# A decoder in split-float products: half of the first FFN by seven block products, one tile of convolution moved to ScalarE and GpSimd

## Chip, core and metric

The kernel runs on one core of a Trainium2 chip. The metric is the time of one execution in microseconds of device time. The kernel before takes 2612.85 us, the median of 3 runs (2611.65 to 2614.08).

## What is computed

A trunk of two layers on 1024 tokens of width 1024, float32 in and out. Layer 0 has a causal depthwise convolution of 31 taps, layer 1 forgetting attention with 16 heads. Both end in an FFN with squared ReLU (inner width 4096) and a per-layer gate.

```python
def layer(i, h):                                  # layer 0: conv, layer 1: attention
    hn = rmsnorm(h, mix_norm[i])
    if i == 0:
        a, g = split(hn @ w_pw1 + b_pw1)
        u = depthwise_causal_conv31(a * sigmoid(g)) + b_dw
        h = h + silu(layernorm(u)) @ w_pw2 + b_pw2
    else:
        h = h + forgetting_attention(hn, w_q, k, v, c) @ w_o   # k, v, c from h
    hn = rmsnorm(h, ffn_norm[i])
    h = h + square(relu(hn @ w1[i])) @ w2[i]      # 1024 -> 4096 -> 1024
    gate = sigmoid(rmsnorm(h, ple_norm[i]) @ w_gate[i])
    return h + gate * (p[i] @ w_proj[i])
```

## The kernel before

Activations lie with channels on the partitions, as 8 tiles of 128 channels, and the tokens in two halves of 512. A product of float32 matrices is made of three matmuls on rounded parts (`mm3`, L132): high by high, high by low, low by high. A weight panel (`panel`, L114) is one 512 KB load into a buffer `raw`, a rounding `wh` on ScalarE, and the remainder `wl = raw - wh`, on GpSimd for half 0 and on VectorE for half 1 (`self.subs`). `work_pools` (L89) gives three buffers each to `wh` and `wl`, and by default two to `raw`. One panel serves 24 matmuls of 128x512 per half. `linear` (L143) runs over panels.

`first` is layer 0. `glu` makes the gated product u; `taps` makes the convolution, per channel tile a sum of 31 shifted products on VectorE (lines L332 to L337, two partial sums `ya`), except the tile in `ONPOOL`, whose products ScalarE makes (`cm`) and GpSimd adds (L324). In this kernel that is done for half 0 alone. `ln_silu` (from L340) has the layer norm: `acc_m`, a mean by matmul `cs_m`, the squares in `acc_ln`, the statistics `st_ln`, `r_ln`, `bc_ln`, then the scaled y and its rounded parts `x1h`, `x1l`. `pw2` (`ps_pw`) is the pointwise product after it. `ffn` works on one half at a time in four chunks of 8 inner tiles: `ps_fa` (into the squared ReLU, parts r) and `ps_fb` (back, added to hT). So one half takes 4 x (192 + 192) matmuls. The gate product (`ple`, `ps_gt`) takes both halves with 8 panels.

The second FFN (`ffn_both`, `ffn_in`, `ffn_out`) makes each 2x2 block product in seven instead of eight block products (`seven`): operands x1 to x7 are sums of quarter blocks of the normalized tokens (`z0f` of half 0, `z1f` of half 1, split into `xf`), weights are combined into `wa` and `wb`; products land in `psa` and `psb`, and sums `e` pass through DRAM (`rd`, `rx`). x1 and x2 need half 0 alone, x5 and the rest need both halves; `tokens_first` and `tokens_rest` make them.

The order on each engine is made by a list scheduler from program order and priorities (`tc.high_priority`), within the limits of the buffers. A pool opened for a later scope takes space that a closed one gave back.

Of the kernel before, what the change touches and what calls it, by code (L numbers as in the profile page):

```python
# [59 lines left out]
class K:  # L60
# [313 lines left out]
    def ffn(self, hT, l, halves=(0, 1), sub=None):  # L374
# [78 lines left out]

    def tokens_rest(self, hT, x, f, hd, gain, name):

        nc = self.nc
        nc.sync.dma_start(hd[1], hT[1].rearrange("p k t -> p (k t)"))
        xd = self.dr.tile([P, 2, 4, HB], F32, name=f"xd_{name}")
        bc = self.stats(hT, 1, name)[1]
        g = self.slot([P, 2, 4, HB], F32, f"z1{name}")  # L460

        def new(p, src):
            t = self.block(f"x{name}{p}")
            x[p] = self.parts(src, t[:, 0], t[:, 1])
# [670 lines left out]
```

## Time and profile before

| what | value |
|---|---|
| median of 3 runs | 2612.85 us (2611.65 to 2614.08) |
| profiled execution, its own time | 2616.24 us |
| its span | 2614.5 us |
| mean granted TensorE clock | 0.969 |
| TensorE busy | 2457.6 us (94%) |
| VectorE busy | 1778.6 us (68%) |
| ScalarE, GpSimd busy | 1078.3 us (41%), 913.1 us (35%) |

The profile is of one execution. The chain of waits is followed from the last instruction back, at each step to what released it; a piece on the chain is time of the kernel, a long busy time beside it is not. Lines are those of the kernel before.

### The profile page before, as it was taken

The page shows a single profiled execution, that of the slowest core. Times are in us where ns is not written, and L with a number is a line of the kernel's source. Part 1 is how long each engine was busy: PE and PEld are TensorE (multiplying, and loading weights), DVE is VectorE, ACT ScalarE, POOL GpSimd, SP SyncE. Part 2 cuts the span into 40 slices and gives each one's busy share as a digit, 9 for nine tenths or more (in the row PEclk, how much of TensorE's full clock was granted, in tenths as well). Part 3 has the DMA queues.
Part 4 walks back from the last instruction along what each step waited for, and adds up shares of the span by engine and source line. Part 5 has one row for each costly group of instructions (what it writes and reads, how often), then busy time and mean ns, then how long its engine had stood idle before and what let it go on. Part 6 is the DMA issues. An engine that isn't in the chain of part 4 may idle for free.

```text
span 2614.5 us, 31465 instructions
## 1 busy us (share of the span) xinstructions
PE 2457.6 (94%) x11672; PEld 2053.1 (79%) x11672; DVE 1778.6 (68%) x2723; ACT 1078.3 (41%) x1670; POOL 913.1 (35%) x747
## 2 busy tenths in 40 slices
PE   7997899999999999989999999798799999999996
PEld 6885678888888888878989898677578887888875
DVE  7999999524744345555686867765877669656655
ACT  5245433233432234334566565643433334333432
POOL 3465544444100000001676665640232323555400
PEclk9998899999999999998999999899799999999987
DMA  3125123222223222222111112314254367443032
GB/s 128 49 71 183 57 78 105 97 97 98 92 89 105 97 97 93 101 83 88 62 57 50 51 49 73 107 59 167 97 208 154 141 212 267 153 145 121 36 125 113
DMA packets 101145, 278.14 MB, mean 106 GB/s; under 512 B 9840, under 2 KB 15600, under 8 KB 99584
## 3 DMA queue, kind: packets, MB, share of 16 engines
q1 hardware_dynamic: 99840, 271.94, 30.1%
q10 hardware_dynamic: 1152, 4.19, 0.4%
q8 instruction: 92, 1.51, 0.2%
q14 instruction: 61, 0.50, 0.1%
HBM read 219.93 MB, written 56.16 MB: 106 GB/s over the span
## 4 chain that ended last, share of the span: by engine, by line
PE 76%; DVE 14%; issue 3%; ACT 3%; POOL 2%; DMA 2%; DVEq 0%; SPq 0%; POOLq 0%; ACTq 0%
PE ps_fb L137 13%; PE ps_fa L137 12%; PE psb L137 9%; PE psa L137 8%; PE ps_gt L137 7%; PE ps_wo L137 3%; PE psq L137 3%; DVE ya L332 3%; PE psv L137 3%; PE pg L137 3%; PE psk L137 3%; PE pa L137 3%; PE po L1002 2%; PE t L1032 2%; PE ps_pw L137 2%
## 5 line engine op out<-in xcount | busy, mean ns | idle before, releaser
L137 PE MATMUL psb<-rx,wb 128*128 128x512 f32 x1344 | 308.3, 392 | 5.7 <-ACT wb L111 5.7
L137 PEld LDWEIGHTS psb<-rx,wb 128*128 128x128 f32 x1344 | 254.0, 189 | 59.5 <-ACT wb L111 6.1
L137 PE MATMUL psa<-xf,wa 128*128 128x512 f32 x1200 | 281.4, 396 | 16.8 <-DVE xf L112 5.5
L332 DVE SCALAR_TENSOR_TENSOR ya<-u,wdw,ya 128x512 f32<-128x512 f32 x420 | 284.2, 747 | 0.0
L137 PEld LDWEIGHTS psa<-xf,wa 128*128 128x128 f32 x1200 | 228.4, 191 | 68.2 <-DVE xf L112 6.6
L111 ACT CAST wh_fb<-raw_fb 128x1024 fp32r<-128x1024 f32 x64 | 67.2, 1053 | 213.3 <-PE ps_fb L137 134.3
L111 ACT CAST wh_fa<-raw_fa 128x1024 fp32r<-128x1024 f32 x64 | 67.3, 1052 | 205.8 <-PE ps_fa L137 114.5
L390 DVE TENSOR_TENSOR hT<-ps_fb,hT 128x512 f32<-128x512 f32 x64 | 44.1, 689 | 147.8 <-PE ps_fb L137 147.8
L984 POOL TENSOR_SCALAR pr<-pr,sm 128x896 f32<-128x896 f32 (+7 forms) x128 | 100.0, 783 | 99.9 <-DVE sm L983 93.7
L205 POOL TENSOR_TENSOR r_g<-ms_g,mhalf 128x4 f32<-128x4 f32 x4 | 5.3, 1327 | 368.2 <-DVE ms_g L203 368.2
L112 DVE TENSOR_TENSOR pt<-t,pt 128x512 fp32r<-128x512 f32 (+1 forms) x160 | 99.2, 634 | 48.6 <-ACT pt L111 47.5
L1002 PE MATMUL po<-pt,V 128*128 128x256 f32 x640 | 121.7, 306 | 10.3 <-ACT pt L111 8.4
L112 POOL TENSOR_TENSOR wb<-rwb,wb 128x1024 fp32r<-128x1024 f32 x32 | 87.2, 2734 | 95.9 <-ACT wb L111 86.6
L982 ACT ACTIVATE pr<-pr,sm 128x896 f32<-128x896 f32 (+7 forms) x128 | 99.3, 776 | 51.9 <-DVE sm L981 35.0
L976 DVE CUSTOM_DVE_ANT_0 pr<-s,pr 128x512 f32<-128x512 f32 (+2 forms) x192 | 103.5, 551 | 22.9 <-POOL pr L963 12.8
L962 POOL TENSOR_SCALAR pr<-cb,ctok 128x896 f32<-128x896 f32 (+7 forms) x128 | 104.9, 826 | 36.1 <-PE t L1032 30.5
L384 DVE SCALAR_TENSOR_TENSOR fa<-ps_fa,bs_f 128x512 f32<-128x512 f32 x64 | 43.8, 689 | 108.4 <-PE ps_fa L137 105.0
L111 ACT CAST pt<-t 128x512 fp32r<-128x512 f32 (+1 forms) x160 | 84.0, 539 | 74.3 <-PE t L1032 70.9
L112 POOL TENSOR_TENSOR wl_fb<-raw_fb,wh_fb 128x1024 fp32r<-128x1024 f32 x32 | 77.4, 2420 | 104.0 <-ACT wh_fb L111 104.0
L112 POOL TENSOR_TENSOR wl_fa<-raw_fa,wh_fa 128x1024 fp32r<-128x1024 f32 x32 | 79.1, 2474 | 90.8 <-ACT wh_fa L111 90.8
L112 DVE TENSOR_TENSOR rx<-rx 128x1024 fp32r<-128x1024 f32 x56 | 79.9, 1437 | 41.8 <-ACT rx L111 41.8
L1002 PEld LDWEIGHTS po<-pt,V 128*128 128x128 f32 x640 | 92.8, 196 | 18.7 <-ACT pt L111 12.4
(362 smaller groups left out, 7094.7 us busy)
## 6 DMA issues: line engine op xcount, KB each, us to landing
raw_fa<-in_wf SPq DMA_DIRECT2D x64, 512.0 KB, 3.4
raw_fb<-in_wf SPq DMA_DIRECT2D x64, 512.0 KB, 3.5
rd<-e SPq DMA_DIRECT2D x112, 256.0 KB, 2.5
rx<-rd SPq DMA_DIRECT2D x28, 1024.0 KB, 5.6
rwa<-in_wf SPq DMA_DIRECT2D x32, 512.0 KB, 4.7
rwb<-in_wf2s SPq DMA_DIRECT2D x32, 512.0 KB, 4.3
raw_gt<-in_wgate SPq DMA_DIRECT2D x24, 512.0 KB, 3.5
proj<-pj SPq DMA_DIRECT2D x32, 256.0 KB, 2.4
```

The costliest lines, as they stand in the source:

```text
L111: copy(h, src)
L112: sub.tensor_tensor(l, src, h.bitcast(F32), ALU.subtract)
L137: self.nc.tensor.matmul(ps, p[:, k, :], q[:, k, :], start=(start and k == k0 and n == 0), stop=(stop and k == kt - 1 and n == 2), skip_gro ...
L332: nc.vector.scalar_tensor_tensor(d, s(j), w(j), o, ALU.mult, ALU.add)
L384: nc.vector.scalar_tensor_tensor(t, ps, 0.0, s[h][1], ALU.max, ALU.mult)
L390: nc.vector.tensor_tensor(hT[h][:, j, :], ps, hT[h][:, j, :], ALU.add)
L962: nc.gpsimd.tensor_scalar(z, cb[:, 0:W], -1.0, self.ctok[:, i, n : n + 1], ALU.mult, ALU.add)
L976: nc.vector.tensor_tensor_reduce(zz, ps[:, 0 : hi - lo], zz, -1.0, 3.0e38, ALU.add, ALU.min, sm[:, m : m + 1])
L982: nc.scalar.activation(z, z, AF.Exp, bias=sm[:, 0:1], scale=-1.0, accum_out=sm[:, 2:3])
L984: nc.gpsimd.tensor_scalar(z, z, sm[:, 3:4], 1.0, ALU.mult, ALU.mult)
L1002: nc.tensor.matmul(po, V[:, j, n % 4, :], pt[:, q, c : c + 256], start=(j == 0 and q == 0), stop=(jp == u and jj == 1 and q == 1),)
L1032: nc.tensor.transpose(ps[:, c : c + P], pr[b][:, j * P : (j + 1) * P], self.ident)
```

## The change

In the first FFN only chunks 0 and 1 (`PLAIN`) stay as they were, for each half. The other 16 inner tiles are made by `ffn_both` with both halves together, with n = 8 and weights stored anew (`wf2s0`). For that the tokens of each half before the FFN are stored to DRAM (`hp`, 2 MB a half) and fetched again, and those after the plain chunks too (`hq`). The plain matmuls fall from 3072 to 1536, and 1344 are added in blocks: 192 fewer in all.

The convolution of half 1 uses `ONPOOL` too: the 32 VectorE instructions of one channel tile become ScalarE products and 30 GpSimd sums. `first` has two pool scopes. The second, with the layer norm, pw2 and plain FFN of half 1, has **one** raw buffer in place of two (and 3 temporaries in place of 4). The gate product of layer 0 takes the halves one after the other, with 16 panel loads in place of 8.

At the end of attention the norm and the operands x1, x2 of half 0 for the second FFN are made in attention's own scope, ahead of the last output products of half 1; and the scope of those last 8 panels has one raw buffer and one temporary.

```diff
+PLAIN = (0, 1)
...
-    def ffn(self, hT, l, halves=(0, 1), sub=None):
+    def ffn(self, hT, l, halves, chunks, sub=None):
...
-        for c in range(NCH):
+        for c in chunks:
...
-            self.linear(a["wf2"][l, c], KT, r, evac2, f"fb{tag}{c}", **kw)
+            self.linear(a["wf2"][c], KT, r, evac2, f"fb{tag}{c}", **kw)
+        return s
...
-    def tokens_first(self, hT, gain, name):
-
-        hd = self.dr.tile([NH, P, KT * HB], F32, name=f"hd_{name}")
-        self.nc.sync.dma_start(hd[0], hT[0].rearrange("p k t -> p (k t)"))
-        bc = self.stats(hT, 0, name)[1]
-        f = self.slot([P, 2, 4, HB], F32, f"z0{name}")
+    def keep(self, dst, hT):
+        self.nc.sync.dma_start(dst, hT.rearrange("p k t -> p (k t)"))
+
+    def tokens_first(self, src, bc, gain, name):
+
+        f = self.slot([P, KT, HB], F32, f"z0{name}")
+        src = self.fetch(f, src)
+        f = f.rearrange("p (i k) t -> p i k t", i=2)
         x = {}
         for p, i in ((1, 0), (2, 1)):
-            self.norm4(f[:, i], hT[0], gain, 4 * i, bc)
+            self.norm4(f[:, i], src, gain, 4 * i, bc)
             t = self.block(f"x{name}{p}")
             x[p] = self.parts(f[:, i], t[:, 0], t[:, 1])
-        return hT, x, f, hd, gain, name
-
-    def tokens_rest(self, hT, x, f, hd, gain, name):
-
-        nc = self.nc
-        nc.sync.dma_start(hd[1], hT[1].rearrange("p k t -> p (k t)"))
+        return x, f, gain, name
+
+    def fetch(self, f, src):
+        if len(src.shape) == 3:
+            return src
+        self.nc.sync.dma_start(f.rearrange("p k t -> p (k t)"), src)
+        return f
+
+    def tokens_rest(self, x, f, gain, name, src, bc):
+
+        nc = self.nc
         xd = self.dr.tile([P, 2, 4, HB], F32, name=f"xd_{name}")
-        bc = self.stats(hT, 1, name)[1]
-        g = self.slot([P, 2, 4, HB], F32, f"z1{name}")
-
-        def new(p, src):
+        g = self.slot([P, KT, HB], F32, f"z1{name}")
+        src = self.fetch(g, src)
+        g = g.rearrange("p (i k) t -> p i k t", i=2)
+
+        def new(p, s):
             t = self.block(f"x{name}{p}")
-            x[p] = self.parts(src, t[:, 0], t[:, 1])
+            x[p] = self.parts(s, t[:, 0], t[:, 1])
...
-            self.norm4(g[:, 1], hT[1], gain, 4, bc)
+            self.norm4(g[:, 1], src, gain, 4, bc)
...
-        self.norm4(g[:, 0], hT[1], gain, 0, bc)
+        self.norm4(g[:, 0], src, gain, 0, bc)
...
-    def ffn_both(self, l, first):
+    def ffn_both(self, l, x, hd, t0, n, w2, rest, pair):
...
-        rd = self.dr.tile([8, 16, P, HB], F32, name=f"rd{l}")
+        rd = self.dr.tile([8, n, P, HB], F32, name=f"rd{l}")
...
-            sp = self.pool(c, f"sw{l}", 2)
-            wr = self.pool(c, f"wr{l}", 4)
-            hT, x, _, hd, gain, name = first
+            sp = self.pool(c, f"sw{l}", 2, side="right")
+            wr = self.pool(c, f"wr{l}", 4, side="right")
...
+                gs = [(0, 1)] if pair else [(0,)]
+                gs += [(g,) for g in range(len(gs[0]), n // 2)]
+                for i, g in enumerate(gs):
+                    for j in g:
+                        load(j)
+                    self.ffn_in(l, g, raw, sp, x, rd, None if i else between)
...
-                for c in range(4):
-                    self.ffn_out(l, c, hT, load_h, wr, wq, sp, rd)
+                for c in range(n // 4):
+                    self.ffn_out(l, c, hT, load_h, wr, wq, sp, rd, w2, c == n // 4 - 1)
...
-                yB = self.taps(u, 1)
+                yB = self.taps(u, 1, ONPOOL)
                 back = tc.cur_priority - p0
             self.sqp = None
+            hp = self.dr.tile([NH, P, KT * HB], F32, name="hp")
+            hq = self.dr.tile([NH, P, KT * HB], F32, name="hq")
             with tc.high_priority(offset=back + 3000):
                 self.pw2(hT, x1, 0)
-                self.ffn(hT, 0, (0,), sub=nc.gpsimd)
-            self.sqp, self.sqt = self.tp, "bc"
+                self.keep(hp[0], hT[0])
+                s0 = self.ffn(hT, 0, (0,), PLAIN, sub=nc.gpsimd)[0]
+                self.keep(hq[0], hT[0])
+        with ExitStack() as c1:
+            self.work_pools(c1, 4, 1, 3)
+            self.psum_pools(c1, 4)
+            self.sqt, self.sqp = "sq", self.pool(c1, "sq0", 3)
             x1 = self.ln_silu(yB, 1)
             self.pw2(hT, x1, 1)
-            self.sqt, self.sqp = "sq", self.pool(c1, "sq0", 3)
-            self.ffn(hT, 0, (1,))
-            self.ple(hT, 0, pj0)
-        return pj1
+            self.keep(hp[1], hT[1])
+            first = self.tokens_first(hp[0], s0[1], "ffn0", "f0")
+            s1 = self.ffn(hT, 0, (1,), PLAIN)[1]
+            self.keep(hq[1], hT[1])
+            late = self.tokens_rest(*first, hp[1], s1[1])
+        hT = self.ffn_both(0, first[0], hq, KT * len(PLAIN), FF // P // 2 - 4 * len(PLAIN), self.a["wf2s0"], lambda: late, False)
+        with ExitStack() as c1:
+            self.work_pools(c1, 5)
+            self.psum_pools(c1, 5)
+            self.sqt, self.sqp = "sq", self.pool(c1, "sq5", 3)
+            self.ple(hT, 0, pj0, (1, 0))
+        return hT, pj1
...
+            hf = self.dr.tile([NH, P, KT * HB], F32, name="hf")
             for k0, k1, h in ((0, KSPLIT, 0), (KSPLIT, NP, 0), (0, KSPLIT, 1)):
                 for _ in self.out_product(k0, k1, (h,), self.at):
                     pass
-                if k0 == 0 and h == 0:
+                if h == 0 and k0 == 0:
                     for p in range(KSPLIT, NP - 1):
                         self.load_o(od, p)
+                elif h == 0:
+                    with tc.high_priority(offset=1):
+                        self.keep(hf[0], self.hn[0])
+                        first = self.tokens_first(self.hn[0], self.stats(self.hn, 0, "f1")[1], "ffn1", "f1")
         with ExitStack() as c3:
-            self.work_pools(c3, 2)
+            self.work_pools(c3, 2, 1, 1)
             self.psum_pools(c3, 2)
             self.sqp = None
-            first = self.tokens_first(self.hn, "ffn1", "f1")
             for _ in self.out_product(KSPLIT, NP, (1,)):
                 pass
-        return first
+        return self.hn, hf, first
...
-        pj1 = k.first(hT)
-        hT = k.ffn_both(1, k.attention(hT))
+        hT, pj1 = k.first(hT)
+        hT, hf, first = k.attention(hT)
+
+        def rest():
+            k.keep(hf[1], hT[1])
+            return k.tokens_rest(*first, hT[1], k.stats(hT, 1, "f1")[1])
+
+        hT = k.ffn_both(1, first[0], hf, 0, 16, a["wf2s1"], rest, True)
```

Three places show how the rows move. The first is TensorE at the end of half 0's plain FFN, around the mean `cs_m` of half 1's layer norm; before:

```order
L137 MATMUL ps_fb_0_4626<-r03h_4298,wl_fb_4623 128x512
L137 MATMUL ps_fb_0_4658<-r03h_4298,wh_fb_4654 128x512
L137 MATMUL ps_fb_0_4658<-r03l_4299,wh_fb_4654 128x512
L349 MATMUL cs_m_4852<-acc_m_4844,meanm 128x512 [waits DVE_49,PE_49]
L137 MATMUL ps_fb_0_4658<-r03h_4298,wl_fb_4655 128x512 [waits Pool_49]
L137 MATMUL ps_fb_0_4658<-r03h_4298,wh_fb_4654 128x512
```

and now, with the statistics and the first matmul of pw2 (`ps_pw_1`):

```order
L141 MATMUL ps_fb_0_3786<-r01l_3267,wh_fb_3782 128x512
L141 MATMUL ps_fb_0_3786<-r01h_3266,wl_fb_3783 128x512
L353 MATMUL cs_m_3840<-acc_m_3832,meanm 128x512 [waits DVE_49]
L193 MATMUL st_ln_3850<-meanm,acc_ln_3851 128x1 [waits DVE_49]
L193 MATMUL st_ln_3850<-meanm,acc_ln_3851 128x1 x3
L162 MATMUL bc_ln_3882<-ident,r_ln_3880 128x128 [waits Pool_49]
L162 MATMUL bc_ln_3882<-ident,r_ln_3880 128x128 x3
L141 MATMUL ps_pw_1_3943<-x1h_3919,wh_pw_3939 128x512 [waits Activation_49]
```

The mean stood among the products of chunk 3; now it stands behind the last product of half 0, and nothing of another stage stands between it and pw2. On VectorE, in the same place, the sum `acc_m` before:

```order
L112 TENSOR_TENSOR r03l_4299<-fa_4547,r03h_4298 128x512 [waits Activation_49]
L384 SCALAR_TENSOR_TENSOR fa_4583<-ps_fa_0_4558,bs_f_2658 128x512 [waits DVE_49,PE_49]
L344 TENSOR_TENSOR acc_m_4844<-y_2072 128x512 [waits DVE_49]
L346 TENSOR_TENSOR acc_m_4844<-acc_m_4844,y_2072 128x512 [waits DVE_49]
L112 TENSOR_TENSOR r03l_4299<-fa_4583,r03h_4298 128x512 [waits Activation_49]
L346 TENSOR_TENSOR acc_m_4844<-acc_m_4844,y_2072 128x512 [waits DVE_49] x5
L390 TENSOR_TENSOR hT_87<-ps_fb_0_4594,hT_87 128x512 [waits PE_49]
L390 TENSOR_TENSOR hT_87<-ps_fb_0_4626,hT_87 128x512 [waits PE_49]
L351 TENSOR_TENSOR y_2072<-y_2072,cs_m_4852 128x512 [waits PE_49]
L351 TENSOR_TENSOR y_2072<-y_2072,cs_m_4852 128x512 x6
```

and now:

```order
L394 TENSOR_TENSOR hT_87<-ps_fb_0_3722,hT_87 128x512 [waits PE_49]
L394 TENSOR_TENSOR hT_87<-ps_fb_0_3754,hT_87 128x512 [waits PE_49]
L394 TENSOR_TENSOR hT_87<-ps_fb_0_3786,hT_87 128x512 [waits PE_49]
L348 TENSOR_TENSOR acc_m_3832<-y_2072 128x512 [waits Pool_49]
L350 TENSOR_TENSOR acc_m_3832<-acc_m_3832,y_2072 128x512 [waits DVE_49] x4
L116 TENSOR_TENSOR wl_pw_3940<-raw_pw_3937,wh_pw_3939 128x1024 [waits DMAHW1_49,Activation_49]
L350 TENSOR_TENSOR acc_m_3832<-acc_m_3832,y_2072 128x512 [waits DVE_49] x2
L355 TENSOR_TENSOR y_2072<-y_2072,cs_m_3840 128x512 [waits PE_49]
```

The sum stood ahead of the last eight additions to hT (two are shown); now it follows the last of them, with a panel's remainder (`wl_pw`) between its pieces.

The second place is SP's queue, which issues the loads, from half 0's last panel on; before:

```order
L120 DMA raw_fb_4812<-in_wf 128x1024 [waits DMAHW0_49,Pool_49]
L120 DMA raw_pw_4949<-in_wpw 128x1024 [waits DMAHW1_49,Pool_49]
L120 DMA raw_pw_4981<-in_wpw 128x1024 [waits DMAHW2_49,Pool_49]
L120 DMA raw_pw_5013<-in_wpw 128x1024 [waits DMAHW3_49,DVE_49]
L120 DMA raw_pw_5045<-in_wpw 128x1024 [waits DMAHW4_49,DVE_49]
L120 DMA raw_pw_5077<-in_wpw 128x1024 [waits DMAHW5_49,DVE_49]
L120 DMA raw_pw_5109<-in_wpw 128x1024 [waits DMAHW6_49,DVE_49]
```

and now:

```order
L124 DMA raw_fb_3780<-in_wf 128x1024 [waits DMAHW5_49,Pool_49]
L124 DMA raw_pw_3937<-in_wpw 128x1024 [waits DMAHW0_49,Pool_49]
L447 DMA hq<-hT_87 128x4096 [waits DMAHW2_49,DVE_49]
L124 DMA raw_pw_3969<-in_wpw 128x1024 [waits DMAHW3_49,DMAHW1_49,DVE_49]
L124 DMA raw_pw_4001<-in_wpw 128x1024 [waits DMAHW4_49,DMAHW3_49,DVE_49]
L124 DMA raw_pw_4033<-in_wpw 128x1024 [waits DMAHW4_49,DVE_49]
L464 DMA z0f_4194<-hp 128x4096 [waits DMAHW6_49,PE_49]
L480 DMA xd_f_5364<-xf_4209 128x2048 [waits DMAHW7_49,Activation_49]
L481 DMA xd_f_5364<-xf_4209 128x2048 [waits DVE_49]
L124 DMA raw_pw_4065<-in_wpw 128x1024 [waits DMAHW5_49,DVE_49]
```

Two-megabyte transfers (`hq`, `z0f`, and `xd` in two parts) now stand between the panels of pw2, and each load after the first waits for VectorE's remainder of the panel before it.

The third place is the start of the second FFN on TensorE; before, from the last output product:

```order
L137 MATMUL ps_wo_15167<-xol_13677,wh_wo_15163 128x512
L137 MATMUL ps_wo_15167<-xoh_13676,wl_wo_15164 128x512
L137 MATMUL psa_010_15210<-xf_15028,wa_15211 128x512 [waits Activation_49]
L137 MATMUL psa_011_15228<-xf_15028,wa_15211 128x512 [waits PE_49]
L137 MATMUL psa_012_15243<-xf_15028,wa_15244 128x512 [waits Activation_49]
L137 MATMUL psa_013_15261<-xf_15028,wa_15244 128x512 [waits DVE_49]
L137 MATMUL psa_010_15210<-xf_15028,wa_15211 128x512 [waits DVE_49]
```

and now:

```order
L141 MATMUL ps_wo_15253<-xol_13763,wh_wo_15249 128x512
L141 MATMUL ps_wo_15253<-xoh_13762,wl_wo_15250 128x512
L141 MATMUL psa_010_15296<-xf_14911,wa_15297 128x512 x12
L141 MATMUL psa_011_15314<-xf_14911,wa_15297 128x512 x12
L141 MATMUL psa_012_15329<-xf_14911,wa_15330 128x512 x12
L141 MATMUL psa_013_15347<-xf_14911,wa_15330 128x512 [waits DVE_49]
L141 MATMUL psa_013_15347<-xf_14911,wa_15330 128x512 x11
L193 MATMUL st_f_15363<-meanm,acc_f_15364 128x1 [waits DVE_49]
```

The first block products went in pieces that waited for operands; now they follow in whole runs, and half 1's statistics (`st_f`) stand behind the first of them. VectorE now has the tokens of half 0 among the output products:

```order
L427 SCALAR_TENSOR_TENSOR z0f_14906<-hTb_13314,vec,bs_f_14904 128x512 [waits Activation_49]
L427 SCALAR_TENSOR_TENSOR z0f_14906<-hTb_13314,vec,bs_f_14904 128x512 x7
L863 TENSOR_TENSOR hTb_13993<-ps_wo_15000,hTb_13993 128x512 [waits PE_49]
L116 TENSOR_TENSOR wl_wo_15066<-raw_wo_15063,wh_wo_15065 128x640 [waits DMAHW4_49,Activation_49]
L116 TENSOR_TENSOR xf_14911<-z0f_14906,xf_14911 128x1024 [waits Activation_49]
L863 TENSOR_TENSOR hTb_13993<-ps_wo_15023,hTb_13993 128x512 [waits PE_49]
L116 TENSOR_TENSOR xf_14911<-z0f_14906,xf_14911 128x1024 [waits Activation_49]
```

`z0f` and the parts `xf` stand between additions of output panels to half 1 (`hTb`) and panel remainders.

## Rows read from the trace of the kernel before

**Rows 1.** Page parts 1 and 4: busy time by engine; the chain by engine.
```profile
PE 2457.6 (94%) x11672; PEld 2053.1 (79%) x11672; DVE 1778.6 (68%) x2723; ACT 1078.3 (41%) x1670; POOL 913.1 (35%) x747
...
PE 76%; DVE 14%; issue 3%; ACT 3%; POOL 2%; DMA 2%; DVEq 0%; SPq 0%; POOLq 0%; ACTq 0%
```

**Rows 2.** Chain of waits, 376 to 730 us: start, us, engine, tile, line, count.
```profile
419.61 43.52 PE ps_fa L137 x192
...
637.21 11.33 PE ps_fb L137 x50
...
684.47 43.60 PE ps_pw L137 x190
```

**Rows 3.** Busy time by stretch: engine busy us (count), granted clock, DMA share, GB/s.
```profile
196.00:261.00 65.00, 46.26 (x195) 36.13 (x193) 61.09 (x84) 38.06 (x62) 36.12 (x23) 0.89 0.53 184
...
392.00:457.00 65.00, 65.00 (x288) 53.86 (x287) 64.67 (x100) 19.83 (x24) 29.37 (x13) 1.00 0.31 103
```

**Rows 4.** VectorE taps, and GpSimd sums of half 0, by tile, 0 to 500 us.
```profile
L332 DVE SCALAR_TENSOR_TENSOR ya<-u,wdw,ya x420: 737/747/755, 48.7 to 486.6; 128x512 f32<-128x512 f32 x140
...
L324 POOL TENSOR_TENSOR y<-y,cm x30: 1261/1294/2370, 167.8 to 224.5; 128x512 f32<-128x512 f32 x30
```

**Rows 5.** Chain of waits, 240 to 285 us: layer norm of half 0.
```profile
243.48 0.59 DVE acc_m L344
...
251.19 2.06 PE cs_m L349 x2
...
268.97 5.36 DVE y L354 x8
...
L137 PE MATMUL ps_pw<-x1h,wh_pw x128: 388/390/797, 276.3 to 727.2; 128*128 128x512 f32 x128
```

**Rows 6.** Panels of the second half's FFN, 728 to 1080 us, by tile.
```profile
L111 ACT CAST wh_fa<-raw_fa x30: 1033/1055/1056, 727.9 to 1018.1; 128x1024 fp32r<-128x1024 f32 x30
L112 DVE TENSOR_TENSOR wl_fa<-raw_fa,wh_fa x30: 1221/1226/1226, 729.0 to 1019.2; 128x1024 fp32r<-128x1024 f32 x30
...
DMA to landing us min/median/max: 3.3/3.4/3.7
```

**Rows 7.** Chain, 1226 to 1262 us, one raw buffer; then DMA issues, 660 to 1240 us.
```profile
1234.62 3.66 DMA raw_wv<-in_wv
...
hd<-hT SPq DMA_DIRECT2D x2, 2048.0 KB, 8.1
...
raw_wv<-in_wv SPq DMA_DIRECT2D x2, 408.0 KB, 4.8
```

**Rows 8.** The same columns as group 3: the second FFN, and the first gate.
```profile
1832.00:1876.20 44.20, 28.24 (x111) 22.91 (x110) 35.44 (x36) 13.14 (x19) 9.85 (x4) 0.77 0.24 95
1876.20:1936.00 59.80, 54.40 (x226) 43.90 (x226) 53.14 (x47) 24.50 (x31) 28.60 (x9) 0.96 0.39 136
2160.00:2200.00 40.00, 33.95 (x141) 26.99 (x140) 36.22 (x37) 17.05 (x19) 13.00 (x6) 0.94 0.94 333
2440.00:2500.00 60.00, 54.43 (x230) 45.07 (x229) 41.98 (x51) 28.27 (x41) 17.12 (x8) 0.89 0.15 51
1080.00:1168.00 88.00, 88.00 (x397) 73.12 (x397) 47.45 (x65) 24.91 (x38) 3.12 (x2) 1.00 0.22 74
```

**Rows 9.** Chain of waits, 1800 to 1945 us: attention's end and second FFN's start.
```profile
1799.86 2.73 PE ps_wo L137 x12
...
1846.74 0.70 DVE acc_f L197
...
1876.23 13.05 PE psa L137 x46
```

**Rows 10.** Panels of attention's last output product, 1798 to 1826 us.
```profile
L111 ACT CAST wh_wo<-raw_wo x8: 495/512/514, 1804.2 to 1817.7; 128x384 fp32r<-128x384 f32 x8
L112 DVE TENSOR_TENSOR wl_wo<-raw_wo,wh_wo x8: 548/558/559, 1804.7 to 1818.6; 128x384 fp32r<-128x384 f32 x8
...
DMA to landing us min/median/max: 2.3/2.4/4.1
```

More of the change, by code (lines that the diff above doesn't have):

```diff
@@ L83, in v, with pool @@
         return self.vec[:, o + k : o + k + 1]
-    def pool(self, ctx, name, bufs, space=None):
+    def pool(self, ctx, name, bufs, space=None, side=None):
         kw = {} if space is None else {"space": space}
+        if side is not None:
+            kw["side"] = side
         return ctx.enter_context(self.tc.tile_pool(name=name, bufs=bufs, reuse_waits="tile", **kw))
@@ L525, in load @@
                         m, q = b // 2, b % 2
+                        r = t0 + 2 * g + n * m
                         nc.sync.dma_start(
-                            raw[g][b],
-                            a["wf1"][l, 2 * g + 16 * m : 2 * g + 16 * m + 2, :, q * HB : (q + 1) * HB]
-                            .rearrange("n p f -> p n f"),
-                        )
-                load(0)
-                load(1)
-                rest = []
+                            raw[g][b], a["wf1"][l, r : r + 2, :, q * HB : (q + 1) * HB].rearrange("n p f -> p n f")
+                        )
+                late = []
                 def between(p):
                     if p == 1:
-                        rest.append(self.tokens_rest(*first))
+                        late.append(rest())
                     elif p == 2:
-                        rest[0]()
-                self.ffn_in(l, (0, 1), raw, sp, x, rd, between)
-                for g in range(2, 8):
-                    load(g)
-                    self.ffn_in(l, (g,), raw, sp, x, rd)
+                        late[0]()
+                gs = [(0, 1)] if pair else [(0,)]
[4 more added lines that the diff above has]
+                    self.ffn_in(l, g, raw, sp, x, rd, None if i else between)
             with ExitStack() as c2:
@@ L613, in ffn_in, with ffn_out @@
         self.seven(w, lambda p: x[p], 2 * len(gs), 4, f"a{l}{gs[0]}", done, between=between)
-    def ffn_out(self, l, c, hT, load_h, wr, wq, sp, rd):
+    def ffn_out(self, l, c, hT, load_h, wr, wq, sp, rd, w2, last):
         nc = self.nc
@@ L643, in done @@
             nc.vector.tensor_tensor(o, ps, o, ALU.add)
-        order = (1, 5, 6, 3, 7, 2, 4) if c == 3 else (1, 2, 5, 6, 3, 7, 4)
+        order = (1, 5, 6, 3, 7, 2, 4) if last else (1, 2, 5, 6, 3, 7, 4)
         self.seven(w, x, 4, 4, f"b{l}{c}", done, order)
@@ L1066, in _panels, with _blocks @@
     ).reshape(m // width, P, kk // P * width)
+def _blocks(w):
+    c = w.shape[0] // D
+    return np.ascontiguousarray(
+        w.reshape(2, c, 4, P, 2, 2, 2, P).transpose(1, 5, 3, 4, 0, 6, 2, 7)
+    ).reshape(c, 2, P, 4, D)
 def _halves(x):
@@ L1096, in prep @@
         "wf1": np.stack([_panels(i["ffn_w1"][l]) for l in range(2)]),
-        "wf2": np.stack([
-            np.stack([_panels(i["ffn_w2"][l, c * D : (c + 1) * D]) for c in range(NCH)]) for l in range(2)]),
-        "wf2s": np.stack([
-            np.ascontiguousarray(
-                i["ffn_w2"][l].reshape(2, 4, 4, P, 2, 2, 2, P).transpose(1, 5, 3, 4, 0, 6, 2, 7)
-            ).reshape(4, 2, P, 4, D) for l in range(2)]),
+        "wf2": np.stack([_panels(i["ffn_w2"][0, c * D : (c + 1) * D]) for c in PLAIN]),
+        "wf2s0": _blocks(i["ffn_w2"][0, len(PLAIN) * D :]),
+        "wf2s1": _blocks(i["ffn_w2"][1]),
         "wq": _panels(i["attn_w_q"][0]),
```

2 lines of the change are left out of this document (1 added, 1 removed).

## The prediction

> **What bounds the kernel now.** I read the page first: TensorE is busy 94% of the span and holds 76% of the chain of waits, VectorE 14% [rows 1]. So matmuls that go are worth their full time wherever TensorE runs without a gap, and nothing where another engine is late. The chain around the first FFN shows such a stretch: 192 matmuls of a chunk take 43.52 us, 0.2267 us each, with no piece of another engine between [rows 2]. The busy time by stretch shows where this is not so: from 196 to 261 us TensorE is busy 46 of 65 us while VectorE, with the convolution, is busy 61; from 392 us TensorE is full, and VectorE still is busy 64.67 of 65 [rows 3]. The kernel has few other holes: one at the start of the second FFN (28.24 of 44.20 us busy) and short ones where a stage of block products ends [rows 8]. The question is thus what the 192 fewer matmuls open in a stage that had no hole.
>
> The sum is made against the profiled execution, 2616.24 us (its span 2614.5 us and 1.7 us around it), which lies 3.4 us above the median 2612.85 us.
>
> **The matmuls.** 192 x 0.2267 = 43.5 us go [rows 2]. Block matmuls have the same shape and are priced alike; what their stages lose is counted below. Term: -43.5.
>
> **The layer norm of half 1.** Before, its sum and mean ran inside chunk 3 of half 0 and cost little: from 637.21 us, where that chunk's second product starts, to 684.47 us, where pw2 starts, it is 47.26 us for 43.52 us of matmuls, 3.7 us lost [rows 2]. Now there is no chunk 3, and `acc_m` follows the last addition to hT on VectorE: TensorE has nothing between the last `ps_fb` and pw2. The same chain of half 0 is the measure: `acc_m` starts at 243.48 us, `cs_m` at 251.19 us, the scaling by the statistics at 268.97 us, and the first `ps_pw` matmul at 276.3 us [rows 5], 32.8 us. In that stretch taps stood between a few pieces; now two or three panel remainders of 1.23 us do [rows 6]. VectorE alone carries the chain, and nothing is queued on TensorE behind the waiting `cs_m` but the statistics and pw2 themselves. I take 33 us with the last addition, and 1.7 us more for slow matmuls after the pause (of pw2 the slowest lasts 797 ns where the median is 390 [rows 5]); less the 3.7 us, +31, from 27 to 36.
>
> **One raw buffer for half 1.** A panel's buffer is held from the issue of its load to the end of its remainder: landing 3.4 us, rounding 1.05 us, remainder 1.23 us [rows 6], some 0.1 us between them, together 5.78 us. TensorE uses up a panel in 24 x 0.2267 = 5.44 us. The loss is 0.34 us a panel, over 8 + 32 panels 14 us; with the 3.66 us of a load in attention, where a raw buffer is single already [rows 7], 0.6 us and 24 us. Against it stand three buffers of finished panels: as a panel ends, its place goes to one whose turn is three panels, 16.3 us, away, and whose conversion, load and conversion take some 8 us; that leaves a lead of 8 us, used up first. But SP's queue has the stores and loads of hp, xd and z1f between the panels: 2 MB land in 8.1 us, and a load behind such a store took 4.8 us though it was smaller than a panel [rows 7]. Four such places at 1.4 to 4.7 us add 6 to 19 us. I take 14 - 8 + 10 = +16, from 0 (the lead lasts) to 34.
>
> The Trainium skill (page "Trainium Kernel Development and Optimization", Best Practices) advises double buffers so that transfers overlap with compute, which speaks against this edit. The trace agrees in part: a load alone, 3.4 us, would hide under 5.44 us of matmuls; it is the two conversions behind it in the same buffer that make the cycle longer than the panel's matmuls.
>
> **The block stage in layer 0.** Three transitions appear. At its start the operands x6, x3, x7, x4 and the sums `e` compete for VectorE; in the second FFN, once all tokens were there, the stretch from 1876.2 to 1936 us has 226 matmuls, 51.2 us of work in 59.8, 8.6 lost [rows 8]. Here x5 is ready sooner: +5 (2 to 9). Where `psa` gives way to `psb` the sums go through DRAM: 141 matmuls in 40 us, 8.0 lost [rows 8]; +8 (6 to 10). Before the gate the second FFN loses 60 - 230 x 0.2267 = 7.9 us [rows 8], while the first gate runs without a hole before (397 matmuls in 88 us) [rows 8]. Its halves now run one after the other, so the first can start while the second is still being added: +6 (2 to 9). Sixteen panels in place of 8, at 24 matmuls each and with two raw buffers, hold 5.44 us as the plain FFN did: 0. Together +19, from 10 to 28.
>
> **The convolution on ScalarE and GpSimd.** 32 x 0.747 = 24 us leave VectorE [rows 4]. But half 0 now has two chunks where it had four to cover half 1's convolution, and the order brings the taps up: ahead of the first `ps_fb` addition of half 0 VectorE's order has 364 of its 448 convolution instructions (both halves), before 359 of 480. Until that place VectorE sets the end [rows 3], so the stage gets nothing from the edit and 5 x 0.747 = 4 us more; after it TensorE is full and the taps are beside the path. +3, from -5 to +6.
>
> A GpSimd sum of that tile takes 1.29 us, at worst 2.37 us, and all 420 taps last 737 to 755 ns, those beside the 30 sums too [rows 4]. The Trainium skill (page "SBUF — State Buffer", section "SBUF: two separate sides") says that a VectorE instruction with two SBUF inputs and a GpSimd instruction that reads SBUF exclude one another for a whole instruction. These rows show GpSimd paying, not the taps; if VectorE paid, it is the third rival.
>
> **The end of attention.** Before, from the last long output product (1802.6 us) to the first product on x5 (1876.23 us) it is 73.6 us, and half 1's `acc_f` starts at 1846.74 us, 29.5 us ahead of it [rows 9]. The tokens of half 0, which stood in between, now run under earlier products. But the last 8 panels have one raw buffer: 0.51 + 0.56 + 2.4 us and gaps are 3.5 us a panel [rows 10], 28 us for 8, against 9 x 0.2267 = 2.04 us of matmuls; and VectorE has eight instructions on block weights ahead of the first of them, at 1.23 us [rows 6] some 10 us. So x5 comes 28 + 29.5 + (0 to 10) = 57 to 67 us after the last long product in place of 73.6: 6 to 16 us gained, with the block weights then ready, and at most the whole loss there, 44.2 - 111 x 0.2267 = 19 us [rows 8]. Term: -12, from -19 to -4. The tokens' own work (8 scalings, 4 splits, 7 additions, some 16 us of VectorE) hides under the long output products; without that cover it would be on the path. Attention's start gains 2 us at most from a first half that is ready sooner: -2, from -5 to 0.
>
> **The sum.** -43.5 + 31 + 16 + 19 + 3 - 12 - 2 = +11.5 us: 2616.24 + 11.5 = 2627.7 us as profiled, 2624 us on the scale of the median. Most of the terms' bounds do not meet at once; the likeliest case reaches from 2613 to 2642 us.
>
> **Rivals.**
> *The covers hold (faster).* The lead of three panels lasts through half 1 (0), the layer norm costs 27, the block stage 10, attention's end gives 19: -43.5 + 27 + 0 + 10 + 3 - 19 - 2 = -24.5, 2588 us. For it: the cycle of a panel exceeds its matmuls by 6% only. Against: the chain of half 0, 32.8 us, has no piece that the change shortens.
> *One raw buffer starves pw2 and the plain FFN (slower by more).* It decides as soon as the loads behind the 2 MB transfers eat the 8 us of lead in pw2: then each panel runs at the loads' pace, +34 in place of +16: 2642 us. For it: SP is one queue in order. Against: loads are in flight together, and 2 MB at 8.1 us leave gaps.
> *GpSimd's sums hold VectorE up.* 30 x 1.29 = 39 us in the stage that VectorE bounds, less the 24 us moved: +15 in place of +3, 2636 us. Against: the taps' 755 ns at most.
> That the change doesn't do what it says is excluded: the order has 2880 matmuls for the first FFN where it had 3072.
>
> **Chances.** 0.47 for the forecast's own case, 0.27 for the covers, 0.16 for starving, 0.10 for GpSimd. A difference within 0.2%, 5.2 us, can't be told from no change. Of the forecast's case a tenth falls below that bound and a quarter within it; the slower rivals lie wholly above it, and of the covers a sixth is within. That makes faster 0.27, same 0.17, slower 0.56. The range for 8 in 10 is 2592 to 2646 us: it leaves out the better tail of the covers and the worse of the starving.
>
> **What would show it.** In the trace of the changed kernel: a hole of some 34 us on TensorE between the last `ps_fb` of half 0 and the first `ps_pw` of half 1, with `acc_m`, `y` and `acc_ln` on the chain; in half 1's plain FFN chunks of 43.5 to 47 us, with the landing of `raw` on the chain if the raw term is right, and 43.5 flat if the covers hold; taps at 0.75 us through the convolution; 5 to 9 us of hole at each end of the block stage; and the first product on x5 of the second FFN 57 to 67 us after the last long output product. The forecast is wrong if the hole at the layer norm is well under 25 us, or if chunks of half 1 run at 43.5 us and attention's end gives back the whole hole.

## The result: 2.6% slower

The changed kernel takes 2680.93 us, median of 4 runs (2675.45 to 2682.64), against 2613.26 us; the ratio is 1.0256 (1.0238 to 1.0274). Forecast were 2624 us, in a range from 2592 to 2646 us. The sign was right, the size was not. The page of the changed kernel, busy time by engine and the chain by engine, answers to [rows 1]:

```profile
PE 2473.9 (92%) x11480; PEld 2022.1 (75%) x11480; DVE 1910.8 (71%) x2816; ACT 1124.0 (42%) x1719; POOL 994.9 (37%) x790
...
PE 65%; DVE 17%; DMA 8%; ACT 4%; issue 3%; POOL 2%; SPq 0%; DVEq 0%; ACTq 0%; POOLq 0%
```

TensorE has 192 matmuls fewer and is busy 16 us longer; DMA holds 8% of the chain where it held 2%. The stages, from starts and ends of their products in both traces:

| stretch | before, us | after, us | change | forecast |
|---|---|---|---|---|
| start to where half 0's first `ps_fb` runs without a pause | 378.7 | 388.9 | +10.2 | +3 |
| end of half 0's second chunk (before: fourth) to end of half 1's pw2, with the 3.7 lost before | 47.3 | 87.1 | +39.8 | +31, and part of +16 |
| half 1's two plain chunks | 176 | 201.5 | +25.5 | the rest of +16 |
| other chunks, now blocks | 350.1 | 323.5 | -26.6 | -24.5 |
| gate to start of `ps_wo` | 642.2 | 638.2 | -4 | -2 |
| `ps_wo` to the last `psb` | 759.7 | 787.9 | +28.2 | -12 |
| last `psb` to the end | 132.7 | 125.4 | -7.3 | 0 |

The rows add up to 66 us, the difference of the two profiled executions (2682.15 and 2616.24 us). What lies between the first row and the second, the rest of that `ps_fb` and half 0's second chunk, is the same in both.

The chain of the changed kernel at half 1's layer norm (start, us, engine, tile, line, count) answers to [rows 5]:

```profile
513.86 2.96 PE ps_fb L141 x13
...
523.55 2.09 PE cs_m L353 x2
...
531.70 3.55 DMA raw_pw<-in_wpw
...
535.27 1.05 ACT wh_pw L115
...
544.36 5.36 DVE y L358 x8
...
559.45 3.98 DVE z0f L427 x6
...
565.35 3.93 DVE xf L116 x4
...
578.37 5.31 DMA raw_pw<-in_wpw
...
586.12 17.79 PE ps_pw L141 x70
```

From the end of `ps_fb` at 516.82 us to the first `ps_pw` at 551.7 us TensorE waits 34.9 us; the forecast said some 34. But a load of a pw2 panel and its rounding are on the chain in the layer norm already (531.70 to 536.32 us), and so are the tokens of half 0 (`z0f`, `xf`) in pw2. Further on, the same view of half 1's plain chunks, against [rows 6]:

```profile
617.15 3.54 DMA raw_fa<-in_wf
620.71 1.06 ACT wh_fa L115
...
621.80 1.24 DVE wl_fa L116
623.05 3.48 DMA raw_fa<-in_wf
...
751.63 7.99 DMA z1f<-hp
...
761.64 3.40 DVE z1f L427 x5
```

Load, rounding and remainder follow one another on the chain, 5.9 us a panel where nothing else comes between, from 610 us almost to the first block product at 805.43 us. From the first load of these chunks to the last (597.86 to 794.28 us) it is 6.3 us a panel on average. The four chunk products take 48 to 55 us each, where 43.5 to 47 were forecast. From 751 to 781 us the fetch of `z1f` and VectorE's work on it stand on the chain in front of the remainders.

At the second FFN, the same view, against [rows 9]:

```profile
1861.78 0.48 DVE wl_wo L116
1862.28 2.30 DMA raw_wo<-in_wo
...
1889.07 11.26 PE psa L141 x48
...
1900.34 0.59 ACT e L600
...
1902.01 0.70 DVE acc_f L201
...
1935.15 2.61 PE psa L141 x10
...
1943.45 8.16 POOL wa L116
```

The last long output product ends at 1854.26 us. The products on x5 go on when its first remainder is there, at 1928.83 us, 74.6 us later (before: at 1876.23 us, 73.6 us later; forecast were 57 to 67), and wait once more for its second remainder, until 1935.15 us. The first of the sums `acc_f` starts 12.9 us after the first block product, behind the 11.26 us of block products and ScalarE's copy `e` of them. It stood so before, too; the chain has there, ahead of `acc_f` at 1846.74 us [rows 9]:

```profile
1845.07 0.58 ACT e L588
```

What no term of the forecast had is in the busy time of a full stretch of second-FFN products: TensorE's busy us and count are the first pair. Before:

```profile
2009.00:2130.00 121.00, 120.76 (x533) 99.75 (x532) 79.61 (x89) 40.70 (x54) 32.27 (x13) 1.00 0.44 159
```

After:

```profile
2060.00:2240.00 180.00, 180.00 (x770) 144.68 (x769) 124.06 (x131) 65.43 (x85) 47.11 (x19) 1.00 0.56 197
```

120.76/533 is 0.2266 us a matmul, 180/770 is 0.2338 us, with a granted clock of 1.00 in both. The shapes are the same.

### The profile page after: what moved, and what is told of

It reads as the page before. It is cut to its first block, busy times and chain, and to the rows that moved or that the text cites. A ratio compares the mean times of both kernels' runs of the same rounds, so it can differ in the third digit from the quotient of the medians.

```text
span 2680.4 us, 31404 instructions
## 1 busy us (share of the span) xinstructions
PE 2473.9 (92%) x11480; PEld 2022.1 (75%) x11480; DVE 1910.8 (71%) x2816; ACT 1124.0 (42%) x1719; POOL 994.9 (37%) x790
## 4 chain that ended last, share of the span: by engine, by line
PE 65%; DVE 17%; DMA 8%; ACT 4%; issue 3%; POOL 2%; SPq 0%; DVEq 0%; ACTq 0%; POOLq 0%
PE psa L141 15%; PE psb L141 15%; PE ps_gt L141 7%; PE ps_fb L141 3%; DVE ya L336 3%; PE pg L141 3%; PE psv L141 3%; PE psk L141 3%; PE psq L141 3%; PE ps_wo L141 3%; PE pa L141 3%; DMA raw_fa<-in_wf 2%; PE po L1033 2%; PE ps_fa L141 2%; PE t L1063 2%
## 5 line engine op out<-in xcount | busy, mean ns | idle before, releaser
L141 PE MATMUL psb<-rx,wb 128*128 128x512 f32 x2016 | 479.7, 400 | 10.5 <-ACT wb L115 7.8
L141 PEld LDWEIGHTS psb<-rx,wb 128*128 128x128 f32 x2016 | 382.8, 190 | 106.5 <-ACT wb L115 9.2
L141 PE MATMUL psa<-xf,wa 128*128 128x512 f32 x1800 | 429.1, 399 | 8.5 <-POOL wa L116 5.0
L141 PEld LDWEIGHTS psa<-xf,wa 128*128 128x128 f32 x1800 | 341.1, 190 | 93.6 <-POOL wa L116 5.4
L116 POOL TENSOR_TENSOR wa<-wt,wa 128x1024 fp32r<-128x1024 f32 x18 | 52.4, 2914 | 460.6 <-ACT wa L115 444.3
L655 DVE TENSOR_TENSOR hTc<-psb,hTc 128x512 f32<-128x512 f32 x168 | 113.9, 684 | 61.4 <-PE psb L141 61.4
L115 ACT CAST rx<-rx 128x1024 fp32r<-128x1024 f32 x84 | 84.1, 1048 | 164.4 <-DMA rx<-rd 164.4
L116 POOL TENSOR_TENSOR wb<-wu,wb 128x1024 fp32r<-128x1024 f32 x36 | 105.0, 2919 | 100.9 <-ACT wb L115 100.9
L116 POOL TENSOR_TENSOR wa<-rwa,wa 128x1024 fp32r<-128x1024 f32 x33 | 83.3, 2525 | 131.9 <-ACT wa L115 131.9
L1063 PE MATMUL t<-ident,pr 128*128 128x128 f32 x576 | 99.2, 283 | 8.4 <-DVE pt L116 5.1
```

The source lines that it names most:

```text
L115: copy(h, src)
L116: sub.tensor_tensor(l, src, h.bitcast(F32), ALU.subtract)
L141: self.nc.tensor.matmul(ps, p[:, k, :], q[:, k, :], start=(start and k == k0 and n == 0), stop=(stop and k == kt - 1 and n == 2), skip_gro ...
L655: nc.vector.tensor_tensor(o, ps, o, ALU.add)
L1063: nc.tensor.transpose(ps[:, c : c + P], pr[b][:, j * P : (j + 1) * P], self.ident)
```

## The experiments

Each is timed against the kernel before on the same chip, in 4 or 5 runs.

**Weights moved by 32 bytes.** In the changed kernel the pool of block weights lies at the right end of SBUF, its large tiles 96 bytes beside a multiple of 128; before they lay on one. These places are those of the program's allocation; the trace shows no addresses.

```diff
+            self.pool(c, f"pad{l}", 1, side="right").tile([P, 8], F32, name=f"pad{l}")
             sp = self.pool(c, f"sw{l}", 2, side="right")
```

> The changed kernel with 32 bytes set aside at the right end of SBUF, so that the weights of the block products (wa, wb) start 32 bytes lower, at a multiple of 64 bytes instead of 32 bytes beside one. Nothing else moves. Theory 1 (the place of the weights in SBUF makes each block matmul slower: 0.2338 us each between 2060 and 2240 us in the changed kernel, 0.2266 us before): the block matmuls go back to 0.2267 us and 4032 x 0.007 = 28 us go, 2653 us (2646 to 2658). Rival (they are slow for another reason, as the far end of SBUF or what runs beside them): nothing changes, 2681 us.

Measured: 2680.11 us, ratio 1.025 (1.0235 to 1.0266), and the products are still slow:

```profile
2060.00:2240.00 180.00, 180.00 (x773) 145.05 (x772) 120.91 (x128) 64.71 (x84) 48.79 (x19) 1.00 0.54 192
```

0.2329 us. The place 64 bytes beside a multiple of 128 is nearly as bad. The theory failed in this form, and the rival stood.

**The opposite in the kernel before.**

```diff
+            self.pool(c, f"pad{l}", 1).tile([P, 8], F32, name=f"pad{l}")
             sp = self.pool(c, f"sw{l}", 2)
```

> The kernel before with the opposite edit: 32 bytes set aside ahead of the weights of the second FFN's block products, so that they start 32 bytes beside a multiple of 64. Theory 1: 2688 x 0.007 = 19 us are added, 2632 us (2628 to 2636), with block matmuls at 0.2338 us. Rival: no change, 2613 us.

Measured: 2625.03 us, 1.0047 (1.0031 to 1.0064): 12 us more, where theory 1 gave 19.

```profile
2009.00:2130.00 121.00, 121.00 (x520) 97.39 (x519) 77.08 (x86) 39.45 (x52) 31.30 (x13) 1.00 0.44 156
```

0.2327 us where 0.2266 stood: the place alone makes them slow, at the left end as well. That contradicts the rival; with the run before it, the multiple must be larger than 64.

**Two raw buffers for half 1.**

```diff
-            self.work_pools(c1, 4, 1, 3)
+            self.work_pools(c1, 4, 2, 3)
```

> The changed kernel with two raw buffers in the scope of half 1's layer norm, pw2 and plain FFN instead of one. Theory 2 (the single buffer's cycle of load, rounding and remainder sets the pace there, and the 2 MB transfers cost only because there is no second buffer): pw2 and the plain FFN of half 1, 255 us from the first pw2 matmul to the first block product, go back to some 220 us; 2681 - 35 = 2646 us (2638 to 2654). Rival (the 2 MB transfers in SP's queue hold the panels up by themselves): only the cycle's 0.4 us a panel go, 2665 us.

Measured: 2623.92 us, 1.0043 (1.0028 to 1.0058): 57 us, more than either theory gave, so two buffers change more than the panels' pace. Its chain:

```profile
503.42 0.79 PE st_ln L193 x8
504.20 6.06 PE ps_fb L141 x26
...
534.35 45.06 PE ps_pw L141 x188
...
624.81 43.52 PE ps_fb L141 x192
668.33 43.52 PE ps_fa L141 x192
```

The plain chunks are back at 43.52 us, and the layer norm's statistics now stand among the products of half 0.

**The convolution of half 1 on VectorE again.**

```diff
-                yB = self.taps(u, 1, ONPOOL)
+                yB = self.taps(u, 1)
```

> The changed kernel with half 1's convolution wholly on VectorE, as before. Theory 3 (GpSimd's sums lengthen VectorE's other instructions in the stage that VectorE bounds: additions of squares 1.68 us where they took 0.90, parts of the FFN operand 1.41 where 0.94; about what the moved tap instructions gave): about the same time, 2675 to 2686 us, since 24 us of taps come back. Rival 3a (the sums cost more than the taps gave): 2665 to 2673 us. Rival 3b (they cost little and the order is what costs): slower by the taps that come back, 2690 to 2705 us.

Measured: 2671.84 us, 1.0221 (1.0206 to 1.0236), 9 us less: rival 3a. What makes the difference is in VectorE's groups from 261 to 392 us (busy us, mean ns). Before:

```profile
L231 DVE SCALAR_TENSOR_TENSOR f00xl<-hT,vec,f00xh 128x512 fp32r<-128x512 f32 x8 | 7.5, 939 | 0.0
L197 DVE TENSOR_TENSOR acc_f<-acc_f,sq_f 128x512 f32<-128x512 f32 x7 | 6.3, 903 | 0.0
...
L332 DVE SCALAR_TENSOR_TENSOR ya<-u,wdw,ya 128x512 f32<-128x512 f32 x92 | 63.6, 746 | 0.0
```

In the changed kernel, with GpSimd's sums beside them:

```profile
L201 DVE TENSOR_TENSOR acc_f<-acc_f,sq_f 128x512 f32<-128x512 f32 x7 | 11.7, 1676 | 0.0
L235 DVE SCALAR_TENSOR_TENSOR f00xl<-hT,vec,f00xh 128x512 fp32r<-128x512 f32 x8 | 11.2, 1405 | 0.0
...
L336 DVE SCALAR_TENSOR_TENSOR ya<-u,wdw,ya 128x512 f32<-128x512 f32 x84 | 57.9, 744 | 0.0
```

In this run, without the sums again:

```profile
L235 DVE SCALAR_TENSOR_TENSOR f00xl<-hT,vec,f00xh 128x512 fp32r<-128x512 f32 x8 | 8.4, 1051 | 0.0
...
L201 DVE TENSOR_TENSOR acc_f<-acc_f,sq_f 128x512 f32<-128x512 f32 x7 | 6.3, 897 | 0.0
```

The additions `acc_f` and the parts `f00xl` together are 9 us longer in the changed kernel and come back but for 1 us; the taps `ya` are the same throughout. The longest of the slow additions, 2.9 us, lie beside a panel remainder on GpSimd with a sum next to it.

**One raw buffer, other places for the temporaries.** In the program, half 1's temporaries begin where the eighth panel buffer of half 0's scope lay; two raw buffers move them off it.

```diff
-            self.work_pools(c1, 4, 1, 3)
+            self.wp, self.raws = self.pool(c1, "wp4", 3), 1
+            self.pool(c1, "gap4", 1).tile([P, 1024], F32, name="gap4")
+            self.tt = self.pool(c1, "tt4", 3)
```

> The changed kernel with one raw buffer still, but 4096 bytes a partition set aside behind the panels of half 1's scope, so that its temporaries lie where they lie with two raw buffers. Two raw buffers took 57 us off the changed kernel, more than the panels' cycle can cost, and their layer norm ran under half 0's last products. Theory 4 (with one buffer the temporaries of half 1's layer norm lie on the last panel buffer of half 0's scope and so come free only after half 0's last product; the order follows from that): the layer norm's hole goes here too, 34 us shrink to some 17, and what is left over two buffers is the panels' cycle alone: 2681 - 20 = 2661 us (2650 to 2665), with the loads still on the chain. Rival (the layer norm waits for the loads of the panels through the single buffer): the hole stays, 2681 us.

Measured: 2665.99 us, 1.02 (1.0181 to 1.0218). Its chain:

```profile
486.98 0.86 PE cs_m L353 x2
487.84 16.36 PE ps_fb L141 x72
...
533.94 1.15 DVE wl_pw L116
535.10 5.28 DMA raw_pw<-in_wpw
...
592.00 9.18 DMA raw_fa<-in_wf
```

The mean runs inside `ps_fb`, and of the hole of 34.9 us 8.1 are left (520.36 to 528.49 us): the rest came from where the temporaries lay. Only 15 us go, since from 535 us on loads are the chain. Against two raw buffers, 2666 - 2624 = 42 us are the single buffer's own. The trace shows where: from the load at 535.10 to that at 783.43 us there are 38 intervals of 6.53 us on average, 41.6 us more than 38 x 5.44. Of these, 24 intervals of at most 6.1 us bring 12 us, and 14 of 6.3 to 11.6 us the other 30. In 10 of the 14 the load took 4 us or more to land; two more stand where VectorE works on the tokens `z1f` and `z0f` between remainders.

**Tokens of half 0 after the plain chunks,** in the kernel just shown.

```diff
-            first = self.tokens_first(hp[0], s0[1], "ffn0", "f0")
             s1 = self.ffn(hT, 0, (1,), PLAIN)[1]
             self.keep(hq[1], hT[1])
+            first = self.tokens_first(hp[0], s0[1], "ffn0", "f0")
```

> The kernel with one raw buffer and the 4096 bytes set aside (2666 us), and in it the tokens of half 0 for the first FFN's blocks (fetch of 2 MB, 8 scalings, 4 splits, two stores) made behind half 1's plain FFN instead of ahead of it in program order; the scheduler puts them among its third chunk product. So nothing stands between pw2's panels on VectorE or in SP's queue but half 0's last store. Theory 6 (VectorE's work on tokens ahead of the panels' remainders, and the transfers, stop the single buffer's cycle as well as the cycle's own length does): pw2 of half 1 becomes shorter by 5 to 10 us, but the same work stands later, so the whole is 2656 to 2664 us. Rival (the cycle's length of 5.9 us for 5.44 us of matmuls is all): 2666 us, the loads on the chain at the same pace.

Measured: 2662.17 us, 1.0181 (1.0164 to 1.0198). pw2 starts 9 us sooner (519.7 against 528.5 us) and takes 49 us instead of 56; of these 16 us 9 are left at the first `psa` (785.2 against 794.6 us) and 4 in the whole, where the runs of the two kernels overlap. So pw2 gains what theory 6 gave, and the time is in its range, but from the first `ps_pw` to the first `psa` it is 265.5 us against 266.1: the work on tokens costs the single buffer as much in the chunks as in pw2. What is left came ahead of pw2, as half 0's last product ends 4.4 us sooner (515.97 us) and the hole is 4.4 us shorter.

**Weights at a multiple of 128 bytes.**

```diff
+            self.pool(c, f"pad{l}", 1, side="right").tile([P, 24], F32, name=f"pad{l}")
             sp = self.pool(c, f"sw{l}", 2, side="right")
```

> The changed kernel with 96 bytes set aside at the right end of SBUF, so that the weights of the block products start at a multiple of 128 bytes. Moving them by 32 bytes off such a place made the block matmuls of the kernel before slow (0.2327 us, 2625 us); moving the changed kernel's to a multiple of 64 only did nothing. Theory 1a (128 bytes is what matters): block matmuls at 0.2267 us, 2681 - 26 = 2655 us (2648 to 2662). Rival (the place at the far end, or the stage, is what makes them slow): 2681 us.

Measured: 2657.28 us, 1.0172 (1.0155 to 1.019): 24 us less.

```profile
2045.00:2215.00 170.00, 169.66 (x749) 140.17 (x748) 112.24 (x119) 60.33 (x79) 45.77 (x18) 1.00 0.52 186
```

0.2265 us, at the far end still: theory 1a holds.

**Two raw buffers for the last output panels.**

```diff
-            self.work_pools(c3, 2, 1, 1)
+            self.work_pools(c3, 2, 2, 1)
```

> The changed kernel with two raw buffers in place of one for the last 8 output panels of attention. Theory 5 (the single buffer's cycle of 3.5 us a panel sets the pace of these 8 panels): the 24.7 us from 1861.8 to 1886.5 us become some 18, and all behind them comes as much sooner: 2674 us (2670 to 2677). Rival (the start of the second FFN waits for something that this does not move): 2681 us.

Measured: 2667.77 us, 1.0212 (1.0196 to 1.0227), 13 us less where 7 were expected. The chain has one piece there in place of 8 cycles:

```profile
1860.36 17.42 PE ps_wo L141 x68
```

**The four together** (two raw buffers twice, 128 bytes, VectorE's convolution).

> The changed kernel with four edits together: two raw buffers for half 1, weights of the block products at a multiple of 128 bytes, half 1's convolution wholly on VectorE, two raw buffers for the last output panels. If their gains add up (57, 26, 9 and 7 us): 2681 - 99 = 2582 us (2574 to 2592), under the kernel before. If the alignment is not what makes the block matmuls slow: 2608 us.

Measured: 2596.64 us, 0.9938 (0.9923 to 0.9953), under the kernel before, but 19 us short of the sum of the four gains, 103 us. Some of it is at the layer norm: with all taps on VectorE the mean stands at 499.45 us (486.98 in the kernel with the gap), the hole between half 0's last product and pw2 is 19.4 us (8.1 with two raw buffers alone), and pw2 runs without a pause from 547.74 us on (534.35 there).

**The same with the moved convolution.**

```diff
-                yB = self.taps(u, 1)
+                yB = self.taps(u, 1, ONPOOL)
```

> The combined kernel (2597 us) with one channel tile of half 1's convolution on ScalarE and GpSimd again, as the change has it. Theory 3a (GpSimd's sums lengthen VectorE's other instructions where VectorE is late): slower by 9 us as in the changed kernel, 2606 us. Rival (with two raw buffers the layer norm of half 1 runs under half 0's products, and it can start sooner when VectorE has 24 us of taps less): the loss is made up, 2590 to 2598 us.

Measured: 2602.74 us, 0.9963 (0.9944 to 0.9981): 6 us slower than without, between theory and rival, and hardly clear of noise, since the two ratios' intervals overlap. Part of the loss is made up at the layer norm, where the hole is 8.1 us again.

**Half 1's statistics first.** In the combined kernel, the statistics are recorded ahead of the first block product.

```diff
+        if between:
+            self.ahead()
         for p in order:
...
+        k.ahead = lambda: None
...
-            return k.tokens_rest(*first, hT[1], k.stats(hT, 1, "f1")[1])
+            return k.tokens_rest(*first, hT[1], k.bs1)
+
+        def ahead():
+            k.bs1 = k.stats(hT, 1, "f1")[1]
+
+        k.ahead = ahead
```

> The combined kernel (2597 us) with half 1's statistics for the second FFN ahead of the first block product's sums in program order, so that ScalarE squares before it copies. Theory 5a (those squares stood in ScalarE's queue behind four copies that wait for the first 48 block matmuls, 11 us): half 1's first addition of squares follows the last output panel at once and the first product on x5 starts some 9 us sooner: 2588 us (2585 to 2593). Rival (GpSimd's remainder of the next weights, 7.9 us, is late next): 2595 us.

Measured: 2579.76 us, 0.9864 (0.985 to 0.9879), 17 us less, where 9 were expected; the fastest here.

```profile
1828.89 2.09 PE bc_f L162 x8
...
1831.62 5.39 DVE z1f L427 x8
...
1863.67 41.55 PE psa L141 x175
```

The broadcast of the statistics stands at 1828.89 us where it stood at 1842.62 us in the combined kernel. The products on x5 begin only 3 us sooner (1853.93 against 1856.64 us), as TensorE now waits for the statistics ahead of the first `psa`, 11 us. The gain lies behind them: from 1863.67 us `psa` runs to the end of this view without a pause, where GpSimd's 7.88 us on weights had stood on the chain behind x5.

## Why the prediction was wrong

As profiled, the kernel got 65.9 us slower where the sum had 11.5. Of the 54 us between, 40 lie from `ps_wo` to the last `psb`, 18 at half 1's layer norm, pw2 and plain chunks, and 7 in the stage of the convolution; the other rows came out 11 us better than forecast. Three steps failed above all: the price of a block matmul, the price of a raw buffer that is alone, and the path to x5 at the end of attention.

*The matmuls.* "Block matmuls have the same shape and are priced alike" failed. The same shape took 0.2338 us with weights 96 bytes beside a multiple of 128 bytes. There are 4032 such matmuls in both FFNs, and the run with 128 bytes took 24 us off. The edit `side="right"` stood in the diff, and no term priced it.

*One raw buffer, +16 from 0 to 34.* It measured 42 us, the kernel with the gap against two raw buffers. The undisturbed cycle was nearly right (5.9 us a panel for the forecast 5.78): 0.46 us more than the matmuls, some 18 us over 40 panels. What failed is what was set against it and beside it. The lead of 8 us was gone at once in pw2, since VectorE scaled and split tokens (559 to 569 us) before the next panel's remainder. And the sum had four disturbed places, at 2 MB transfers, where the trace of the kernel with the gap has 14: with one buffer every load that lands late and all work of VectorE ahead of a remainder delays the next load. The rival that the buffer starves the stage named this, and priced it at +34.

*The layer norm, +31.* The hole of 34.9 us was sized right, in part by luck: 4.6 us of it are a panel's load and rounding, which the term did not have. Its cause was not the missing chunks by themselves, but temporaries that lay on a buffer of half 0's panels. The kernel with the gap has the same two chunks and a hole of 8.1 us. But there the single buffer is late next, and only 15 us come back. The cover that two chunks give is short all the same: in the combined kernel, where VectorE has all taps and the layer norm starts later, the hole is 19.4 us without this cause. The two terms together were +47, and the rows of the two stages measured 65; two raw buffers take 50 of them back at the first `psa` (755.2 against 805.3 us), 57 in the whole.

*The convolution, +3 from -5 to +6.* The stage lost 10 us. The order was read rightly, that it brings the taps up; the rival in which GpSimd holds VectorE up was nearer. The taps indeed did not pay; other VectorE instructions did, and the rows chosen [rows 4] were of taps alone. A tap was the wrong witness: its sum `ya` lies in PSUM (the pool `yp`), so it reads one 128x512 tensor from SBUF, while `acc_f` and `f00xl` read two. The Trainium skill (page "SBUF — State Buffer", section "SBUF: two separate sides") says that VectorE instructions with two SBUF inputs and GpSimd instructions that read SBUF exclude one another. The trace agrees: the additions took 1676 ns for 903, the parts 1405 for 939, and the taps 744 for 746. Nor does GpSimd pay beside taps, as the prediction read its 1.29 us: in the changed kernel, from 287 to 372 us, a sum beside taps alone takes 1.27 to 1.31 us, close to the least there is (1.26), and beside the other two groups up to 2.35 us.

*The block stage, +19.* 323.5 - 304.7 = 18.8 us, but by chance: with aligned weights the stage takes 314.4 us, so its transitions cost 10, the low end of 10 to 28, and the slow matmuls 9.

*The end of attention, -12.* It measured +28 from `ps_wo` to the last `psb`. 18 of it are slow matmuls (770.1 us with aligned weights). The single buffer of the output panels cost 13 us by its run; 3.5 us a panel was right, and with it this wait was foreseen. The path to x5 measured 34.8 us for the panels (forecast 28 to 38), 26.8 from `acc_f` to x5 (29.5), and between them 12.9 us that the sum put at nothing: half 1's squares stand behind ScalarE's copies `e`, which wait for the first block products. GpSimd's 8 us on weights after x5 were not foreseen either. The order of VectorE and TensorE had been read there, ScalarE's had not. In the kernel with the statistics first, which has two raw buffers and aligned weights as well, `ps_wo` to the last `psb` takes 746.8 us, 13 less than before; how much of that the earlier tokens give isn't told apart.

Why the last stretch is 7 us shorter stays open.

## What to carry to other kernels

Before a saving in matmuls is counted, look at where the change puts each operand and each temporary: 32 bytes decided 3% of every block matmul, and a reused buffer decided most of whether a layer norm was hidden. A buffer that is held through load and conversions should be priced with everything that stands ahead of its last reader on that reader's engine, not with its own cycle alone. Where a chain is moved, read the order on every engine it passes, ScalarE's too. And where one instruction is to stand for others beside a busy GpSimd, see in which memory its operands lie.

## What was not expected of the hardware

The time of a 128x512 matmul with weights loaded anew each time depended on the byte where the weights start in a partition: a multiple of 128 bytes 0.2266 and 0.2265 us, 32 bytes beside it 0.2327, 64 beside it 0.2329, 96 beside it 0.2338 us. These are counts in a window; from start to start of neighbours in the same five traces it is 0.2267 us on the multiple, 0.2333 at 32 and at 64 bytes beside it, 0.2343 at 96. Only TensorE's operand matters here: what else moved with it, raw weights and in one kernel the sums, TensorE doesn't read. Which of the weight loads or the matmuls pays isn't told apart by these rows: loads took 187.5 ns a piece before and 188.1 after.
